# A decoder block: input projection as 22 Strassen pairs, then attention beside twelve gate blocks

## The chip, the core and the metric

The kernel runs on one core of a Trainium2 chip. Its engines work side by side and wait for each other by semaphores: TensorE (PE) multiplies matrices into PSUM, VectorE (DVE), ScalarE (ACT) and GpSimd (POOL) do the elementwise work, and SyncE (SP) issues DMAs. Each engine, and SP's queue, takes its instructions in a fixed row. The metric is the device time of one execution in microseconds; lower is better.

## The reference

One layer over 1040 positions (16 meta tokens and 1024 real ones), model width 1024, all in float32:

```python
h = xn @ w_in                                   # 1024 -> 8 * 1024
b_c, c_c, h_c, q, k, v, g_conv, g_attn = split(h)
y_conv = b_c * causal_dwconv(c_c * h_c, conv_w_mix)
z = q @ k.T / 8                                 # 16 heads of 64
log_beta = log_sigmoid(z)
log_fail = where(s < t, log_beta - z, 0)
survive = reverse_cumsum(log_fail) - log_fail
a = where(s < t, exp(log_beta + survive), 0)    # stick-breaking weights
o = a @ v
merged = sigmoid(g_conv + b0) * (y_conv @ w_proj_conv) \
       + sigmoid(g_attn + b1) * (o @ w_proj_attn)
x = x + rms_norm(merged @ w_out)
u, g = split(rms_norm(x) @ w_up_gate)
x = x + rms_norm((gelu(causal_dwconv(u)) * g) @ w_down)
```

A weight a[t,s] is beta(s) times the product of fail = 1 - beta over the positions between s and t. With P(s) the product of fail from s up, a[t,s] = P(s+1) - P(s), so o is also the sum over s of P(s) (v(s-1) - v(s)) plus the last v.

## The kernel before

Every float32 operand of a matmul is split into a high part (cast to float32r, by ACT) and a low part (the difference, by DVE or POOL), and a product is three matmuls: high x high, high x low, low x high. Weights come in blocks of 128 output features. A dense block (an *item* of `Dense`) loads its weights (`raw`), makes `whi` (ACT, L110) and `wlo` (POOL, four pieces, L113), and runs three chunks of about 342 tokens: 3 x 8 x 3 = 72 matmuls (L129 to L131) into a PSUM tile `mm`.

The input projection has 64 such items: 8 each of q, k, v, 24 of the convolution (c, h, b) and 16 gates. They are written between the steps of attention. `stage1` makes for each head and each block of 114 queries the scores (`z`, L330 and L331), two sigmoids (`fl` = fail, L332; `be` = beta, L333), the running product of `fail` (a scan on DVE, L340), beta times the product (POOL, L346) and the mask (POOL, L348). `stage2` transposes the weights (`tp`, L377), splits them (`ah` on ACT, `al` on DVE) and multiplies by v (`av`, L367 and L368). q, k and v of a head pair stay in SBUF. Two cost tables (`COST1`, `COST2`) and `marks` set how many dense steps stand between two steps of attention; what gates are left follow behind it. Then come the two branch projections (their inputs `yT` and `oT` are loaded from DRAM through a ring of two `ld` tiles and split), the output projection, the up/gate projection and the down projection.

The up/gate projection already works in Strassen form. Two weight blocks and both halves of the input dimension make a 2x2 block matrix, the even and odd tokens the other; with the operands A11, S1 to S4, A12, A22 of weights and B11, T1 to T4, B21, B22 of tokens there are seven products in place of eight. Its matmuls (L863, L865, L867) go into `st` tiles.

Of the kernel before, what the change touches and what calls it, by code (L numbers as in the profile page):

```python
# [1 line left out]

# [29 lines left out]

@with_exitstack
def block_kernel(ctx, tc, x, meta_tokens, g_pre_mix, w_in, channels, w_proj_conv,
# [23 lines left out]
    m_d = tc.dram_tile([D, NQ], F32, name="m_d")  # L58
    mm_d = tc.dram_tile([7, P, KB * QB], F32, name="mm_d")
# [4 lines left out]
    def split(hi, lo, src, lo_engine=None):  # L64
        nc.scalar.copy(hi, src)  # L65
        (lo_engine or nc.vector).tensor_tensor(lo, src, hi.bitcast(F32), op=ALU.subtract)  # L66

# [13 lines left out]
    class Dense:  # L81


        def __init__(self, pspool, items):
            self.ps = pspool
            self.items = items
            self.raw, self.hl = {}, {}
            self.i, self.gen, self.total, self.later = 0, None, 0, []

        def defer(self, n, fn):  # L90
            self.later.append((self.total + n, fn))

# [48 lines left out]
        def step(self):  # L141
            while self.i < len(self.items):
# [17 lines left out]
    def col_block(w, c):  # L160
# [51 lines left out]
    CH_C = [(T0 - 2, CH + 2), (T0 + CH, CH), (T0 + 2 * CH, CH)]  # L212
    CH_K = [(0, T0 + CH), (T0 + CH, CH), (T0 + 2 * CH, CH)]

    QH, QL, KK, V = {}, {}, {}, {}

    def item_q(p):
        def evac(ci, a, n, ps):
            if ci == 0:
                QH[p] = [heads.tile([P, NQ], F32R, name="qh", tag="qh") for _ in range(2)]  # L220
                QL[p] = [heads.tile([P, NQ], F32R, name="ql", tag="ql") for _ in range(2)]
                for h in range(2):
                    z0 = 64 * (1 - h)
                    nc.gpsimd.memset(QL[p][h][z0:z0 + 64, :].bitcast(F32), 0.0)
            c = slice(a - T0, a - T0 + n)
            for h in range(2):
                own, other = slice(64 * h, 64 * h + 64), slice(64 - 64 * h, 128 - 64 * h)
                hi, lo = QH[p][h], QL[p][h]
                nc.scalar.copy(hi[own, c], ps[own])
                nc.vector.tensor_copy(hi[other, c], ps[own])  # L230
                nc.vector.tensor_tensor(lo[own, c], ps[own], hi[own, c].bitcast(F32), op=ALU.subtract)
        return (col_block(w_in, 24 + p), src_x, CH_Q, evac)

    def item_k(p):
        def evac(ci, a, n, ps):
            if ci == 0:
                KK[p] = [heads.tile([P, NT], F32R, name="kk", tag="kk") for _ in range(2)]
            c = slice(a, a + n)
            for h in range(2):
                own, other = slice(64 * h, 64 * h + 64), slice(64 - 64 * h, 128 - 64 * h)  # L240
                k = KK[p][h]
                nc.scalar.copy(k[own, c], ps[own])
                nc.vector.tensor_tensor(k[other, c], ps[own], k[own, c].bitcast(F32), op=ALU.subtract)
        return (col_block(w_in, 32 + p), src_x, CH_K, evac)

    def item_v(p):
        st = {}

        def evac(ci, a, n, ps):
            if ci == 0:  # L250
                st["vt"] = work.tile([P, NT], F32, name="vt", tag="wk", bufs=4)
            vt = st["vt"]
            nc.scalar.copy(vt[:, a:a + n], ps)
            if ci < 2:
                return
            vv = heads.tile([P, 9, 2, P], F32R, name="vv", tag="vv", bufs=2)
            V[p] = vv

            def tokens(k0, kn, m):
                tp = ps_tp.tile([P, 512], F32, name="tp", tag="tp")  # L260
                for k in range(kn):
                    s0 = KEYS[k0 + k][0]
                    nc.tensor.transpose(tp[:m, k * P:(k + 1) * P], vt[:, s0:s0 + m], ident)
                tv = tp[:m, :kn * P].rearrange("p (k h d) -> p k h d", k=kn, h=2)
                split(vv[:m, k0:k0 + kn, :, 0:64], vv[:m, k0:k0 + kn, :, 64:128], tv)

            dense.defer(1, lambda: tokens(0, 4, P))
            dense.defer(2, lambda: tokens(4, 4, P))
            dense.defer(3, lambda: tokens(8, 1, QB))
        return (col_block(w_in, 40 + p), src_x, CH_K, evac)  # L270

    def items_conv(cb):
        st = {}

        def evac_c(ci, a, n, ps):
            if ci == 0:
                st["c"] = work.tile([P, NT], F32, name="cc", tag="wk", bufs=4)
            nc.scalar.copy(st["c"][:, a - 12:a - 12 + n], ps)

        def evac_h(ci, a, n, ps):  # L280
            c = st["c"][:, a - 12:a - 12 + n]
            nc.vector.tensor_tensor(c, c, ps, op=ALU.mult)
            if ci == 2:
                st["y"] = work.tile([P, NT], F32, name="yy", tag="wk", bufs=4)
                conv3(st["y"][:, :NQ], st["c"], NQ, lambda k: w_mix(k, cb))

        def evac_b(ci, a, n, ps):
            y = st["y"][:, a - T0:a - T0 + n]
            nc.vector.tensor_tensor(y, y, ps, op=ALU.mult)
            if ci == 2:  # L290
                nc.sync.dma_start(y_d[cb * P:(cb + 1) * P, :], st["y"][:, :NQ])

        return [(col_block(w_in, 8 + cb), src_x, CH_C, evac_c),
                (col_block(w_in, 16 + cb), src_x, CH_C, evac_h),
                (col_block(w_in, cb), src_x, CH_Q, evac_b)]
# [13 lines left out]
    gp = {"p": work, "n": 4}  # L309

    def gate_pool():
        return gp["p"]

    COST1, COST2 = (726.0, 1752.0, 2778.0), (1000.0, 1900.0, 2800.0)

    def stage1(p, h, g):
        res = []
        qh, ql, kk = QH[p][h], QL[p][h], KK[p][h]
        for b in range(3 * g, 3 * g + 3):
            nk = P + QB * b  # L320
            q0 = QB * b
            fl = work.tile([P, NT], F32, name="fl", tag="fl")[:QB]
            be = work.tile([P, NT], F32, name="be", tag="be", bufs=6)[:QB]
            nch = -(-nk // 512)
            wch = 2 * (-(-nk // (2 * nch)))
            c0 = 0
            while c0 < nk:
                n = min(wch, nk - c0)
                z = ps_z.tile([P, 512], F32, name="z", tag="z")[:QB, :n]
                nc.tensor.matmul(z, qh[:, q0:q0 + QB], kk[:, c0:c0 + n], start=True, stop=False)  # L330
                nc.tensor.matmul(z, ql[:, q0:q0 + QB], kk[:, c0:c0 + n], start=False, stop=True)  # L331
                nc.scalar.activation(fl[:, c0:c0 + n], z, AF.Sigmoid, scale=-0.125)  # L332
                nc.scalar.activation(be[:, c0:c0 + n], z, AF.Sigmoid, scale=0.125)  # L333
# [901 lines left out]
```

## Time and profile before

| | us |
|---|---|
| median of 3 runs | 2027.31 (2026.77 to 2027.63) |
| profiled execution | 2019.99 |
| its span | 2018.2 |
| PE busy | 1968.4 |
| DVE, ACT, POOL busy | 1006.3, 853.3, 1022.7 |
| first matmul of the first branch projection starts at | 1014.2 |

The span is that of one profiled execution. A busy time is the time in which an engine has an instruction under way; matmuls overlap, so a busy PE may still be waiting inside. A group's row reads: line, engine, operation, output <- inputs, shapes, count, then busy time and mean duration of one in ns, then the idle time of the engine before them and who ended it.

### The profile page before, as it was taken

The numbers are of one execution on the slowest core, as the hardware profiler recorded it, in microseconds if no ns is written. First come the engines' busy times: TensorE is split into PE (matmuls) and PEld (weight loads), VectorE is DVE, ScalarE is ACT, GpSimd is POOL, SyncE is SP. The second block draws the span as 40 slices with busy tenths as digits, with TensorE's granted clock in tenths as the row PEclk, the third lists the DMA queues.
The fourth block names the chain that finished last, engine by engine and source line by source line (L and its number), as shares of the span: only waits on it lengthen the run. The fifth ranks groups of instructions, "written<-read, shape, count | busy, mean of one in ns | idle before, by whom it ended". The sixth has DMA issues, their size and how long they took to land.

```text
span 2018.2 us, 30990 instructions
## 1 busy us (share of the span) xinstructions
PE 1968.4 (98%) x12228; PEld 1857.0 (92%) x12228; DVE 1006.3 (50%) x1545; ACT 853.3 (42%) x1771; POOL 1022.7 (51%) x1062
## 2 busy tenths in 40 slices
PE   6999999999999999999999999979999999999997
PEld 6999999999999999999999999969988998888886
DVE  6445555555555555553341126874354445345546
ACT  5544555555454545555421123453443344321122
POOL 2643666565555646565223550345556565654353
PEclk9999999999999999999999999989999999999998
DMA  3111101111111111012664673303121212253223
GB/s 137 43 63 43 53 32 64 43 53 43 42 53 43 58 39 62 32 64 73 189 221 156 188 214 114 97 31 126 63 84 67 102 66 82 92 174 111 84 84 136
DMA packets 56174, 177.58 MB, mean 88 GB/s; under 512 B 12872, under 2 KB 12872, under 8 KB 56028
## 3 DMA queue, kind: packets, MB, share of 16 engines
q1 hardware_dynamic: 52704, 165.09, 24.5%
q10 hardware_dynamic: 3324, 10.50, 1.7%
q8 instruction: 96, 1.57, 0.3%
q14 instruction: 50, 0.41, 0.1%
HBM read 131.36 MB, written 44.21 MB: 87 GB/s over the span
## 4 chain that ended last, share of the span: by engine, by line
PE 87%; DVE 7%; ACT 2%; DMA 2%; POOL 1%; issue 1%; ACTq 0%; DVEq 0%; SPq 0%; POOLq 0%
PE mm L129 14%; PE mm L130 14%; PE mm L131 14%; PE st L863 7%; PE st L867 7%; PE st L865 7%; PE tp L377 3%; PE st L1157 3%; PE st L1155 3%; PE st L1156 3%; PE av L368 2%; PE av L367 2%; PE z L331 2%; PE z L330 2%; PE po L706 1%; PE po L708 1%
## 5 line engine op out<-in xcount | busy, mean ns | idle before, releaser
L129 PE MATMUL mm<-xnT,whi 128*128 128x342 f32 (+2 forms) x1536 | 505.5, 329 | 0.3 <-ACT xnT L65 0.2
L130 PE MATMUL mm<-xnT,whi 128*128 128x342 f32 (+2 forms) x1536 | 494.0, 322 | 0.5 <-DVE xnT L66 0.5
L131 PE MATMUL mm<-xnT,wlo 128*128 128x342 f32 (+2 forms) x1536 | 492.3, 320 | 0.0
L346 POOL TENSOR_TENSOR be<-be,fl 114x271 f32<-114x271 f32 (+14 forms) x288 | 206.0, 736 | 310.3 <-DVE fl L340 301.6
L113 POOL TENSOR_TENSOR wlo<-raw,whi 128x256 fp32r<-128x256 f32 x320 | 254.8, 828 | 208.2 <-ACT whi L110 207.3
L130 PEld LDWEIGHTS mm<-xnT,whi 128*128 128x128 f32 x1536 | 291.0, 189 | 2.1 <-DVE xnT L66 1.0
L129 PEld LDWEIGHTS mm<-xnT,whi 128*128 128x128 f32 x1536 | 290.2, 189 | 2.9 <-ACT xnT L65 0.8
L131 PEld LDWEIGHTS mm<-xnT,wlo 128*128 128x128 f32 x1536 | 290.0, 189 | 0.0
L340 DVE TENSOR_TENSOR_SCAN fl<-fl,upper 114x128 f32<-114x128 f32 (+2 forms) x144 | 214.4, 1490 | 112.2 <-ACT fl L332 64.0
L66 POOL TENSOR_TENSOR a_op<-raw,a_op 128x512 fp32r<-128x512 f32 (+1 forms) x136 | 193.7, 1437 | 87.9 <-ACT a_op L65 85.6
L66 DVE TENSOR_TENSOR al<-tp,ah 114x342 fp32r<-114x342 f32 (+3 forms) x288 | 128.3, 452 | 148.8 <-ACT ah L65 147.5
L65 ACT CAST ah<-tp 114x342 fp32r<-114x342 f32 (+3 forms) x288 | 113.0, 398 | 165.3 <-PE tp L377 157.0
L863 PE MATMUL st<-opT,a_op 128*128 128x258 f32 (+2 forms) x528 | 172.3, 326 | 3.2 <-ACT snap L878 1.8
L865 PE MATMUL st<-opT,a_op 128*128 128x258 f32 (+2 forms) x528 | 170.1, 322 | 2.6 <-DVE opT L66 1.7
L867 PE MATMUL st<-opT,a_op 128*128 128x258 f32 (+2 forms) x528 | 170.0, 322 | 0.0
L332 ACT ACTIVATE fl<-z 114x348 f32<-114x348 f32 (+10 forms) x240 | 111.4, 464 | 123.6 <-PE z L331 93.5
L65 ACT CAST a_op<-raw 128x512 fp32r<-128x512 f32 (+1 forms) x136 | 85.1, 634 | 156.0 <-DMA raw<-in_w_up_gate_dram 51.8
L1162 DVE TENSOR_TENSOR acc<-acc,st 128x512 f32<-128x512 f32 x144 | 98.5, 687 | 91.1 <-PE st L1157 91.1
L865 PE MATMUL st<-opB,a_op 128*128 128x512 f32 (+2 forms) x396 | 127.6, 322 | 0.0
L863 PE MATMUL st<-opB,a_op 128*128 128x512 f32 (+2 forms) x396 | 127.6, 322 | 0.0
L867 PE MATMUL st<-opB,a_op 128*128 128x512 f32 (+2 forms) x396 | 127.2, 321 | 0.0
L377 PE MATMUL tp<-ident,be 114*114 114x114 f32 (+1 forms) x720 | 118.5, 262 | 4.1 <-DVE al L66 3.4
(168 smaller groups left out, 4320.5 us busy)
## 6 DMA issues: line engine op xcount, KB each, us to landing
raw<-in_w_in_dram SPq DMA_DIRECT2D x64, 512.0 KB, 3.3
raw<-in_w_up_gate_dram SPq DMA_DIRECT2D x44, 512.0 KB, 3.3
act_d<-owork SPq DMA_DIRECT2D x22, 512.0 KB, 4.3
araw<-act_d SPq DMA_DIRECT2D x22, 512.0 KB
raw<-in_w_down_dram SPq DMA_DIRECT2D x22, 512.0 KB, 3.3
y_d<-yy SPq DMA_DIRECT2D x8, 513.0 KB
ga_d<-gt SPq DMA_DIRECT2D x8, 513.0 KB
o_d<-ot SPq DMA_DIRECT2D x8, 513.0 KB
```

Of the source, the lines that this page charges most:

```text
L65: nc.scalar.copy(hi, src)
L66: (lo_engine or nc.vector).tensor_tensor(lo, src, hi.bitcast(F32), op=ALU.subtract)
L113: nc.gpsimd.tensor_tensor(lo[:, c], raw[:, c], hi[:, c].bitcast(F32), op=ALU.subtract)
L129: nc.tensor.matmul(ps, wh, xh, start=(kb == 0), stop=False)
L130: nc.tensor.matmul(ps, wh, xl, start=False, stop=False)
L131: nc.tensor.matmul(ps, wl, xh, start=False, stop=(kb == KB - 1))
L340: nc.vector.tensor_tensor_scan(fl[:, :nk][:, ::-1], fl[:, :nk][:, ::-1], upper[:, NT - nk:][:, ::-1], 1.0, op0=ALU.mult, op1=ALU.max)
L346: nc.gpsimd.tensor_tensor(be[:, a:e], be[:, a:e], fl[:, a + 1:e + 1], op=ALU.mult)
L377: nc.tensor.transpose(tp[:n, QB * j:QB * (j + 1)], blocks[j][0][:, k0:k0 + n], ident[:QB, :QB])
L863: nc.tensor.matmul(ps, wt[:, 0, k], xh, start=start and kb == 0, stop=False, skip_group_check=True)
L865: nc.tensor.matmul(ps, wt[:, 0, k], xl, start=False, stop=False, skip_group_check=True)
L867: nc.tensor.matmul(ps, wt[:, 1, k], xh, start=False, stop=stop and kb == 3, skip_group_check=True)
```

## The change

Three parts, all ahead of the branch projections.

1. *A Strassen stage.* After the norm and five plain blocks, 44 of the 64 blocks run as 22 pairs, in two halves of 260 tokens. The token operands T1 to T4 are made once (`tops`); B11, B21, B22 are parts of `xnT`. q, k and v are stored to DRAM as high and low parts. v is turned into differences v(s-1) - v(s) (`dv`) and transposed; the last v of each query block is kept in `ends`.
2. *Attention beside 12 gate blocks.* Heads load q, k (64 partitions at a time) and v from DRAM, three heads ahead at most. Scores, one sigmoid, the scan, transposes of the scan itself, split, products with the differences, and at the end an addition of `ends`. Beta, its product and the mask are gone. Two gates (`late_gates`) follow as `Dense` items while the eight `y` blocks are loaded.
3. *A list scheduler.* Each step is a task of `Plan` with an engine, a cost, a key and the slots that it takes and frees; `run` writes them out in the order in which they would start. `in_program_order` keeps that order on every engine.

```diff
+class Plan:
+    LAG = {"PE": 0.22, "ACT": 0.1, "DVE": 0.1, "POOL": 0.1, "SP": 3.5, None: 0.0}
...
+    plan = Plan({"raw": 2, "whi": 0, "wlo": 0, "ap": 4, "wk": 5, "st": 8, "xw": 2})
...
+            h = plan.add("ACT", act_cost(n), high, tuple(after), key + 3, ("wk",))
+            t = plan.add("DVE", dve_cost(n), lower, (h,), key + 4)
+            s1 = plan.add("SP", 0.4, lambda: nc.sync.dma_start(hi_d[rows, :], st["hi"].bitcast(F32)), (h,), key + 4)
...
+            nc.vector.tensor_tensor(st["dv"][:, 1:], u()[:, :NT - 1], u()[:, 1:], op=ALU.subtract)
...
+                for kb in range(4):
+                    c = slice(kb * P, (kb + 1) * P)
+                    xh, xl = token_op(tok, kb, s * HS, HS)
+                    nc.tensor.matmul(ps, wt[:, 0, c], xh, start=start and kb == 0, stop=False,
+                                     skip_group_check=True)
+                    nc.tensor.matmul(ps, wt[:, 0, c], xl, start=False, stop=False, skip_group_check=True)
+                    nc.tensor.matmul(ps, wt[:, 1, c], xh, start=False, stop=kb == 3, skip_group_check=True)
...
+    FL = [2] * 6 + [1] * 3
+    plan = Plan({"raw": 2, "whi": 1, "wlo": 1, "mm": 2, "z": 2, "tp": 3, "av": 1, "qk": 3, "vv": 2,
+                 "ot": 2, "wk": 2, "ah": 4, "al": 4, "half": 1, **{f"fl{b}": n for b, n in enumerate(FL)}})
...
+    share = {0: 0.18, 1: 0.33, 2: 0.49}
...
+    DELAY = 0.6 * half_pair
...
+                            nc.scalar.activation(bst["fl"][:, c0:c0 + n], bst["z", c0], AF.Sigmoid,
+                                                 scale=-0.125)
...
+                        nc.vector.tensor_tensor_scan(fl[:, ::-1], fl[:, ::-1], upper[:, NT - nk:][:, ::-1],
+                                                     1.0, op0=ALU.mult, op1=ALU.max)
...
+                            nc.tensor.transpose(tp[:n, QB * j:QB * (j + 1)], fls[b]["fl"][:, k0:k0 + n],
+                                                ident[:QB, :QB])
...
+            nc.gpsimd.tensor_tensor(ov, ov, ends[:, p].unsqueeze(2).to_broadcast([P, 9, QB]), op=ALU.add)
...
+    items = [item_gate(0, ob) for ob in late_gates]
-                    nc.gpsimd.tensor_tensor(be[:, a:e], be[:, a:e], fl[:, a + 1:e + 1],
-                                            op=ALU.mult)
```

How the rows of instructions move, at three places. First PE, in the middle of the input projection. Before, dense matmuls of 342 columns stand with a pair of scores (`z`) between them:

```order
L330 MATMUL z<-kk,qh 114x470
L331 MATMUL z<-kk,ql 114x470
L129 MATMUL mm<-xnT,whi 128x342
L130 MATMUL mm<-xnT,whi 128x342
L131 MATMUL mm<-xnT,wlo 128x342
```

In the change, PE's row there holds only Strassen products of 260 columns; the place is the step from B22 (a part of `xnT`) to T4 (`tT_504`) as the token operand:

```order
L776 MATMUL st<-xnT,s_op 128x260
L778 MATMUL st<-xnT,s_op 128x260
L779 MATMUL st<-xnT,s_op 128x260
L776 MATMUL st<-tT_504,s_op 128x260
L778 MATMUL st<-tT_504,s_op 128x260
L779 MATMUL st<-tT_504,s_op 128x260
```

No score, transpose of weights or weighted sum is left in that part of the row. Second, DVE inside attention. Before, the scans (`fl`) and the low parts (`al`) stand among the splits of q that the projection needs:

```order
L340 SCALAR_TENSOR_TENSOR fl<-fl,upper 114x698
L66 TENSOR_TENSOR al<-tp,ah 128x342
L66 TENSOR_TENSOR al<-tp,ah 114x228
L230 CAST qh<-mm 64x342
L231 TENSOR_TENSOR ql<-mm,qh 64x342
L66 TENSOR_TENSOR al<-tp,ah 114x114
```

In the change, near the end of attention, DVE's row has nothing but these two kinds:

```order
L975 SCALAR_TENSOR_TENSOR fl<-fl,upper 114x698
L429 TENSOR_TENSOR al<-tp,ah 114x342 x2
L429 TENSOR_TENSOR al<-tp,ah 114x228
L975 SCALAR_TENSOR_TENSOR fl<-fl,upper 114x812
L429 TENSOR_TENSOR al<-tp,ah 114x114
L429 TENSOR_TENSOR al<-tp,ah 128x342
L975 SCALAR_TENSOR_TENSOR fl<-fl,upper 114x926
```

The splits of q and k have moved into the stage before. Third, PE at the end of attention. Before, three dense matmuls stand behind each transpose and its pair of weighted sums:

```order
L377 MATMUL tp<-ident,be 114x114 x3
L367 MATMUL av<-ah,vv 128x342
L368 MATMUL av<-al,vv 128x342
L129 MATMUL mm<-xnT,whi 128x342
L130 MATMUL mm<-xnT,whi 128x342
L131 MATMUL mm<-xnT,wlo 128x342
```

In the change the last of the twelve gates has ended some hundred rows earlier, and single matmuls of the next gate stand between:

```order
L994 MATMUL tp<-ident,fl 114x114 x6
L1009 MATMUL av<-ah,vv 128x342
L1010 MATMUL av<-al,vv 128x342
L994 MATMUL tp<-ident,fl 114x114 x2
L1009 MATMUL av<-ah,vv 128x342
L233 MATMUL mm<-xnT,wlo 128x342
L1010 MATMUL av<-al,vv 128x342
L994 MATMUL tp<-ident,fl 114x114
```

The dense matmuls that stood beside the last units of attention now stand ahead of them, or behind.

More of the change, by code (lines that the diff above doesn't have):

```diff
@@ L246, in item_v @@
[L246 to L295, printed above, removed]
+    HT = NT // 2
@@ L414, in block_kernel, with plain_step @@
[L414 to L431 removed]
+    def plain_step(ps, hi, lo, kb, a, n):
+        k = slice(kb * P, (kb + 1) * P)
+        xh, xl = src_x(kb, a, n)
+        nc.tensor.matmul(ps, hi[:, k], xh, start=(kb == 0), stop=False)
+        nc.tensor.matmul(ps, hi[:, k], xl, start=False, stop=False)
+        nc.tensor.matmul(ps, lo[:, k], xh, start=False, stop=(kb == KB - 1))
@@ new lines, in block_kernel, with load_raw, whole @@
+    ends = xnt_pool.tile([P, NPAIR, 9], F32, name="ends")
+    gates = [(1, ob) for ob in range(8)] + [(0, ob) for ob in range(8)]
+    N_FIRST, N_LATE = 1, 2
+    strassen_gate, bridge_gate = gates[0], gates[1]
+    mid_gates = gates[2:16 - N_LATE]
+    late_gates = [ob for _, ob in gates[16 - N_LATE:]]
+    def load_raw(o):
+        raw = wpool.tile([P, D], F32, name="raw", tag="raw")
+        nc.sync.dma_start(raw, w_in[o])
+        return raw
+    def whole(raw):
+        hi = wpool.tile([P, D], F32R, name="whi", tag="whi")
+        lo = wpool.tile([P, D], F32R, name="wlo", tag="wlo")
+        return hi, lo
@@ new lines, in late_tile, with plain_out, make, evac @@
+    def late_tile(u):
+        return lambda: u["t"]
+    def plain_out(done, k, t0):
+        u = {}
+        def make():
+            u["t"] = wk_tile("su")
+        def evac(a, n, ps):
+            nc.scalar.copy(u["t"][:, a:a + n], ps)
+        return make, evac, lambda after, key: done(k, late_tile(u), after, key)
+    done_q, done_k = done_qk(qh_d, ql_d, T0), done_qk(kh_d, kl_d, 0)
+    block = {}
+    for k in range(8):
+        block["v", k] = (40 + k, k, done_v)
+        block["q", k] = (24 + k, k, done_q)
+        block["k", k] = (32 + k, k, done_k)
+        block["c", k] = (8 + k, k, done_c)
+        block["h", k] = (16 + k, k, done_h)
+        block["b", k] = (k, k, done_b)
@@ new lines, in block_kernel @@
+    at = 0.0
+    item = 24 * 3 * pe_cost(CH)
+    for i, name in enumerate((("v", 0), ("q", 0))):
+        u = {"t": first_out[i]}
+        o, k, done = block[name]
+        plain(o, CH_K, at, None, lambda a, n, ps, u=u: nc.scalar.copy(u["t"][:, a:a + n], ps),
+              lambda after, key, done=done, k=k, u=u: done(k, late_tile(u), after, key), bank,
+              2, (*first_ops[i], None))
+        at += item / 3
+    for name in (("k", 0), ("v", 1), ("q", 1)):
+        o, k, done = block[name]
+        plain(o, CH_K, at, *plain_out(done, k, 0), bank)
+        at += item
@@ new lines, in block_kernel, with gate_out, make, evac @@
+    snap_free = {}
+    for i in range(len(pairs1)):
+        strassen_pair(i, at)
+        at += 14 * prod
+    def gate_out(which, ob, tile_of, space):
+        u = {}
+        def make():
+            u["t"] = tile_of()
+        def evac(a, n, ps):
+            nc.scalar.activation(u["t"][:, a - T0:a - T0 + n], ps, AF.Sigmoid, bias=bias_gate(which, ob))
+        def finish(after, key):
+            plan.add("SP", 0.4, lambda: nc.sync.dma_start(
+                (gc_d, ga_d)[which][ob * P:(ob + 1) * P, :], u["t"][:, :NQ]), tuple(after), key, (), space)
+        return make, evac, finish
@@ new lines, in block_kernel, with next_load, next_high @@
+    which, ob = bridge_gate
+    plain(48 + 8 * which + ob, CH_Q, at, *gate_out(which, ob, lambda: wk_tile("gt"), ("wk",)), bank)
+    at += item
+    nxt = {}
+    which, ob = mid_gates[0]
+    def next_load():
+        nxt["raw"] = load_raw(48 + 8 * which + ob)
+    def next_high():
+        nxt["hi"], nxt["lo"] = whole(nxt["raw"])
+        nc.scalar.copy(nxt["hi"], nxt["raw"])
+    ld = plan.add("SP", 0.4, next_load, (), at - 20, ("raw",))
+    h = plan.add("ACT", act_cost(D), next_high, (ld,), at - 10, ("whi", "wlo"))
@@ new lines, in block_kernel @@
+    plan.join([plan.add("POOL", pool_cost(256), lambda j=j: lo_piece(nxt["raw"], nxt["hi"], nxt["lo"], j),
+                        (h,), at - 9) for j in range(4)], ("raw",))
+    plan.run()
+    psS.close()
+    t_ctx.close()
+    early_ctx.close()
+    psA = ctx.enter_context(ExitStack())
+    ps_mm = psA.enter_context(pool("ps_mm", 2, space=PSUM))
+    ps_z = psA.enter_context(pool("ps_z", 2, space=PSUM))
+    ps_tp = psA.enter_context(pool("ps_tp", 3, space=PSUM))
+    ps_av = psA.enter_context(pool("ps_av", 1, space=PSUM))
@@ L540, in block_kernel @@
+    plan.run()
+    last = len(nc.cur_bb.bb.instructions)
+    psA.close()
+    work_ctx.close()
+    heads_ctx.close()
+    psB0 = ctx.enter_context(ExitStack())
+    items = [item_gate(0, ob) for ob in late_gates]
+    n_gates = len(items)
+    dense = Dense(psB0.enter_context(pool("ps_mmB", 3, space=PSUM)), items)
     slots_abc = ctx.enter_context(ExitStack())
```

814 lines of the change are left out of this document (590 added, 224 removed).

## The prediction, as it stood before the run

> **What bounds the kernel now.** I read the page's busy shares and its chain first, then the stages by windows, then the groups that the change touches.
>
> ```profile
> PE 1968.4 (98%) x12228; PEld 1857.0 (92%) x12228; DVE 1006.3 (50%) x1545; ACT 853.3 (42%) x1771; POOL 1022.7 (51%) x1062
> PE 87%; DVE 7%; ACT 2%; DMA 2%; POOL 1%; issue 1%; ACTq 0%; DVEq 0%; SPq 0%; POOLq 0%
> ```
>
> TensorE is busy 98% of the span and carries 87% of the chain that ended last. The windows (span from:to, length, then busy time and count of PE, PE's weight loads, DVE, ACT, POOL, then clock, DMA share, GB/s) say where:
>
> ```profile
> 0.00:45.00 45.00, 29.14 (x170) 26.61 (x170) 30.52 (x77) 25.57 (x54) 11.18 (x19) 1.00 0.43 154
> 45.00:925.00 880.00, 874.52 (x5782) 855.48 (x5781) 471.35 (x685) 454.75 (x1037) 499.81 (x654) 1.00 0.14 49
> 925.00:970.00 45.00, 44.54 (x299) 43.62 (x298) 17.64 (x25) 21.41 (x46) 22.21 (x28) 1.00 0.19 68
> 970.00:1014.00 44.00, 44.00 (x282) 44.00 (x281) 11.93 (x24) 18.56 (x40) 11.54 (x16) 1.00 0.75 226
> 1340.00:1770.00 430.00, 426.89 (x2645) 381.66 (x2645) 194.68 (x233) 179.29 (x305) 248.28 (x180) 1.00 0.24 85
> ```
>
> From 45 to 1014 us, all of the input projection and the attention, PE idles 6 us (5.5 + 0.5). So only fewer PE cycles can make this part shorter; work taken off DVE, ACT or POOL there is worth nothing by itself. The last row is the up/gate projection, already in Strassen form: 22 pairs, and PE idles 3.1 us in 430. It is the model for the new stage.
>
> **Removed and added PE work.** A matmul's listed duration overlaps the next one's, so I price by the distance of starts:
>
> ```profile
> 1000.04 0.32 PE L129 MATMUL mm<-xnT,whi 128*128 128x342 f32 x1
> 1007.89 0.32 PE L131 MATMUL mm<-xnT,wlo 128*128 128x342 f32 x1
> 1499.76 0.28 PE L863 MATMUL st<-opB,a_op 128*128 128x256 f32 x1
> 1504.34 0.28 PE L867 MATMUL st<-opT,a_op 128*128 128x256 f32 x1
> L129 PE MATMUL mm<-xnT,whi 128*128 128x342 f32 (+2 forms) x1536 | 505.5, 329 | 0.3 <-ACT xnT L65 0.2
> ```
>
> Between the first two rows lie 50 steps: 7.85/50 = 0.157 us for 342 columns. Between the next two lie 38: 4.58/38 = 0.1205 us for 256. The slope, 0.0365/86 = 0.0004 us a column, gives 0.122 us for 260. Three lines of 1536 matmuls are 64 blocks of 72. Of these, 44 go: 3168 x 0.157 = 497.4 us, and 2 us more, since key and value blocks have 14 extra columns in their first chunk. In come 22 pairs x 7 products x 2 halves x 12 = 3696 matmuls of 260 columns: 3696 x 0.122 = 451 us (bounds 445 at the 256-column price, 455 with 1 ns more each). PE saving: **48 us** (44 to 54).
>
> The Trainium skill ("TensorE: Matmul & The Clock Gate", Back-to-back issue gap) gives N/2.4 + 2.5 ns for an isolated warm stream, 145 and 111 ns here; by it the saving would be 459 - 410 = 49 us. The trace's pitches are 8 to 10% longer, and they are used.
>
> Transposes, scores and weighted sums keep their counts (720, 480, 576), so they cancel. Their size is still needed. Busy time to 1014 is 29.1 + 874.5 + 44.5 + 44.0 = 992; less the blocks (4608 x 0.157 + 2 = 725) that is 267. About 15 us of it are the 144 other transposes at the 0.105 us found below, so attention's PE work is some 250 us, and the new attention stage with its 12 gate blocks (12 x 72 x 0.157 = 136) has **386 us** for PE.
>
> **Work on other engines.**
>
> ```profile
> L346 POOL TENSOR_TENSOR be<-be,fl 114x271 f32<-114x271 f32 (+14 forms) x288 | 206.0, 736 | 310.3 <-DVE fl L340 301.6
> L333 ACT ACTIVATE be<-z 114x348 f32<-114x348 f32 (+10 forms) x240 | 110.6, 461 | 0.0
> L348 POOL TENSOR_SCALAR_AFFINE_SELECT be<-be 114x114 f32<-114x114 f32 x144 | 113.6, 789 | 10.1
> L340 DVE TENSOR_TENSOR_SCAN fl<-fl,upper 114x128 f32<-114x128 f32 (+2 forms) x144 | 214.4, 1490 | 112.2 <-ACT fl L332 64.0
> L66 DVE TENSOR_TENSOR al<-tp,ah 114x342 fp32r<-114x342 f32 (+3 forms) x288 | 128.3, 452 | 148.8 <-ACT ah L65 147.5
> L113 POOL TENSOR_TENSOR wlo<-raw,whi 128x256 fp32r<-128x256 f32 x320 | 254.8, 828 | 208.2 <-ACT whi L110 207.3
> ```
>
> The second sigmoid (110.6 us on ACT), the multiplication and the mask (206.0 + 113.6 us on POOL) go, replaced by differences of v and a sum of ends. Directly that is worth 0: PE hid them. Indirectly it is what lets attention fit beside 386 us of PE. There DVE keeps scans and low parts, 214.4 + 128.3 = 343 us: 89% of the stage, where its share was 54% (471 of 880).
>
> *Strassen stage.* Each pair asks of POOL seven low parts and of DVE four combinations and six evacuations, as in the model stage, plus the q/k/v splits and the convolution. The model's PE waits were 3.1 us; I take 4 (3 to 12: the convolution and splits share the ring of output tiles, and a late store would hold an evacuation). The token operands T1 to T4 are made under 264 plain matmuls, 264 x 0.157 = 41 us; nearly free.
>
> *Attention stage.* The old one idled 5.5 us in 880, with DVE at 54%. At the same rate 386 us would lose 2.4 us; at 89% there is little slack when a scan is late, and the queue behind it is the low part that releases a transpose bank, for which PE waits. I take 8 (2 to 30).
>
> *q/k/v through DRAM.* Head 0's six loads wait for the last T4 product. Until the first score PE has 72 + 39 = 111 gate matmuls, 17.4 us.
>
> ```profile
> L553 SPq DMA_DIRECT2D ld<-y_d x8: 319/320/424, 973.4 to 997.4; - x8
> DMA to landing us min/median/max: 4.6/5.6/6.7
> L65 ACT CAST yT<-ld x24: 473/477/480, 978.7 to 1003.1; 128x342 fp32r<-128x342 f32 x24
> L129 PE MATMUL mm<-yT,whi x192: 315/318/327, 1014.2 to 1103.9; 128*128 128x342 f32 x192
> ```
>
> Six issues of 0.32 and a landing of 5.6 are 7.5 us; on SP they stand behind the last store of the Strassen gate, a few us more. Hidden, unless the gate block ahead of them runs short; I take 2 for all the joints (0 to 10). Later heads have three buffers.
>
> *The end of attention.* Before, gate matmuls stand between all of its last products. Now, after the last mid gate, PE's row has 11 score pairs, 66 transposes, 27 weighted pairs and seven strays of the next gate. DVE has seven scans and 26 low parts.
>
> ```profile
> 890.65 0.32 PE L131 MATMUL mm<-xnT,wlo 128*128 128x342 f32 x1
> 890.81 0.46 PE L377 MATMUL tp<-ident,be 114*128 114x114 f32 x3
> 891.04 0.40 PE L129 MATMUL mm<-xnT,whi 128*128 128x342 f32 x1
> 891.28 0.32 PE L130 MATMUL mm<-xnT,whi 128*128 128x342 f32 x1
> L340 DVE TENSOR_TENSOR_SCAN fl<-fl,upper 114x1040 f32<-114x1040 f32 x16 | 40.1, 2508 | 16.3 <-POOL be L346 9.7 <-ACT fl L332 6.5
> L340 DVE TENSOR_TENSOR_SCAN fl<-fl,upper 114x356 f32<-114x356 f32 x16 | 17.5, 1092 | 8.9 <-ACT fl L332 8.9
> ```
>
> Two dense matmuls and three transposes take 0.63 us, so a transpose is (0.63 - 0.314)/3 = 0.105. PE: 66 x 0.105 = 6.9, scores of 9772 columns 4.5, weighted sums 7.3, strays 1.1: 19.8 us. DVE: scans between 1.09 and 2.51, about 1.8 x 7 = 12.6, and 26 x 0.452 = 11.8: 24.4 us, and some 2 us from the last low part to the last sum. PE idles 24.4 + 2 - 19.8 = **7 us** (3 to 17; the upper end is half a microsecond of waiting for ACT before each of 20 low parts).
>
> *The projection behind it.* The eight y blocks took from 973.4 to about 1004.4, 31 us, under five gate blocks. Now only two gates (21.5 us after the strays) stand behind attention. Two loads are issued early (one landing saved, 6); the others stand on SP behind the last store of o, which waits for POOL's last addition (4 more). Ready at 31 - 6 + 4 = 29; PE needs the last block at 21.5 + 7 x 3 x 0.157 = 24.8. Wait: **5 us** (0 to 12).
>
> **Sum.** -48 (PE work) - 6 (old idle) + 4 + 8 + 2 + 7 + 5 = **-28 us**. The profiled execution took 2019.99 (span 2018.2), 7.3 below the median of 2027.31; the same difference goes to the median: **2000 us**.
>
> **Rivals.**
> - *The waits hide.* Strassen 3, attention 2, tail 3, the rest 0: -54 + 8 = -46, 1981 us. For it: PE's 0.6% idle in the old mix. Against it: the old mix kept dense matmuls to the end.
> - *The joints are dearer.* Tail 12, y 10, joints 8 in place of 14: -12, 2015 us. For it: where PE last ran beside a DVE chain, its clock fell too:
>
> ```profile
> 1310.00:1330.00 20.00, 11.43 (x66) 10.67 (x67) 16.98 (x28) 8.71 (x14) 3.29 (x2) 0.74 0.08 24
> ```
>
>   PE busy 57% had a granted clock of 0.74. The Trainium skill ("TensorE: Matmul & The Clock Gate", Part 1: The HAM clock gate) says that an idle window of about 3.4 us halves the clock; 925 to 970 shows none, the next tail may.
> - *Slower: DVE becomes the bound by waiting in its row.* In the old kernel it waited 147.5 us for ACT's high parts. If its fixed row in the new stage keeps these waits, the stage takes 343 + 147.5 = 490 us against 386 + 8: +96 - 28 = +68, 2095 us. It decides from 343 + waits > 394 + 28, that is 79 us of waits. Against it: there DVE had nothing else to do, and scans now stand between.
> - *Slower: POOL locks DVE out.* POOL has 44 weight pieces x 0.83, 48 half additions and 8 last ones, some 105 us by the same rate per column. Taken one after the other with DVE: 343 + 105 = 448, +54 - 28 = +26, 2053 us. Such delays are in the rows already, with POOL at 57% (500 of 880), where it now has 27%. The Trainium skill ("SBUF — State Buffer", Who interferes with whom) has a lock between a DVE operation with two SBUF inputs, as the scan is, and a GpSimd operation that reads SBUF; the low parts, one input from PSUM, are outside it.
>
> **Chances.** Forecast (1988 to 2008) 0.45, waits hide 0.22, dearer joints 0.21, DVE bound 0.07, lock 0.05. What counts as no change is within 0.2%, 4 us. Faster: 0.45 + 0.22 + 0.18 of the joints = 0.85; same 0.04; slower 0.11. The range reaches from below the hidden case to beyond the joints, 1976 to 2024, and leaves out the two slower rivals and a little at each end.
>
> **What would show it.** A 22-pair stretch of some 455 us with PE idle under 12; an attention stretch of 390 to 405 us with DVE near 85% busy; 5 to 10 us of PE gaps at its end; PE waiting for yT at the first projection block; this block starting near 986 instead of 1014. PE waits on al or fl spread over the whole attention stretch, or scans much above 1.5 us on average, would make the prediction wrong.

## The result, and the profile after

The changed kernel takes 2015.35 us (median of 4 runs, 2014.96 to 2017.75), the kernel before 2027.04 (4 runs, 2025.46 to 2027.63): a ratio of 0.9946, 95% interval 0.9929 to 0.9963. It is faster by 11.7 us where 28 were forecast; 2015 was the time of the rival with dearer joints. The profiled execution took 2014.96 (span 2012.9).

The page's busy shares and its chain, after:

```profile
PE 1921.6 (95%) x12756; PEld 1806.6 (90%) x12756; DVE 1089.6 (54%) x1585; ACT 842.1 (42%) x1774; POOL 907.7 (45%) x676
PE 73%; DVE 12%; ACT 3%; POOL 3%; DMA 2%; issue 2%; ACTq 0%; DVEq 0%; SPq 0%; POOLq 0%
```

TensorE's share fell from 98% to 95%: there is less work for it, and it waits more. DVE has gone from 7% to 12% of the chain. The stages by windows (span, length, then busy time and count of PE, weight loads, DVE, ACT, POOL, clock, DMA share, GB/s); 585.6 is the first score, 981.3 the last weighted sum, 1003.0 the first projection matmul:

```profile
0.00:45.00 45.00, 28.98 (x171) 27.01 (x172) 28.75 (x74) 25.00 (x54) 7.38 (x15) 1.00 0.42 154
45.00:585.60 540.60, 517.48 (x4142) 514.77 (x4141) 268.23 (x320) 208.26 (x424) 292.16 (x208) 0.98 0.36 111
585.60:981.30 395.70, 375.94 (x2610) 357.12 (x2608) 310.83 (x432) 261.82 (x669) 124.92 (x102) 1.00 0.49 128
981.30:1003.00 21.70, 21.70 (x140) 21.70 (x140) 5.65 (x12) 9.10 (x20) 5.66 (x6) 1.00 0.62 174
```

PE idles 540.6 - 517.5 = 23.1 us up to attention and 395.7 - 375.9 = 19.8 in it. Who ended those waits, up to the first score (engine, line, waited for: total, times, longest):

```profile
PE st L776 <- ACT tT L638: 8.1, 1, 8.1
PE st L569 <- DVE dv L553: 4.7, 1, 4.7
PE st L776 <- ACT snap_e L786: 4.5, 6, 0.9
PE st L331 <- ACT whi L439: 2.5, 1, 2.5
PE st L333 <- POOL wlo L354: 2.5, 1, 2.5
PE st L778 <- POOL tT L429: 0.8, 1, 0.8
```

and from there to the projection:

```profile
PE av L1010 <- DVE al L429: 11.4, 20, 1.8
PE tp L994 <- DVE al L429: 6.0, 6, 1.3
PE mm L231 <- ACT yT L158: 2.6, 1, 2.6
```

The first table is the surprise: 4.5 us in it are the running Strassen stage, waiting for snapshots. The other 18.6 are one place, between 52 and 103 us, where the token operands T1 to T4 are made. Two of these waits (`whi`, `wlo`, 5.0) are still in the plain blocks; ACT and POOL have casts and low parts of token operands ahead of them in their rows. Then PE, three quarters through its first product with T1, waits 8.1 + 0.8 for T1's last quarter, and 4.7 for `dv`.

The cause stands in DVE's row:

```profile
44.72 4.62 DVE L612 TENSOR_TENSOR xa<-xnT 128x1040 f32<-128x1040 f32 x2
49.27 3.53 DVE L162 TENSOR_TENSOR xa<-xa 128x520 f32<-128x520 f32 x2
```

and in POOL's, at the same time:

```profile
44.88 6.75 POOL L617 TENSOR_TENSOR xb<-xnT 128x1040 f32<-128x1040 f32 x2 [24.68 <-DVE xnT L159]
```

Two additions of 1040 columns take DVE 4.62 us and POOL 6.75 beside each other. Later in the same row a single one takes DVE 1.23 (at 92.64, with POOL idle). A subtraction of 520 columns takes 0.69 where POOL is idle as it starts and 1.2 to 2.8 where it is not. In all, DVE's 28 operations on token operands take 38 us, where 4 x 1.23 + 24 x 0.69 make 21.5. And DVE stands still for POOL, 6.0 us in three waits for low parts, of which POOL makes one in 1.3 us where it is alone:

```profile
DVE xa L162 <- POOL tT L429: 6.0, 3, 2.5
```

The cover is shorter than planned, too. Line L331 has one of every three plain matmuls here:

```profile
44.00:83.50 39.50, 21.36 (x64) 12.45 (x64) 0.91 0.24 83
121.34 0.33 PE L331 MATMUL st<-xnT,whi 128*128 128x356 f32 x1
```

Only 3 x 64 = 192 of the 264 plain matmuls run before the first Strassen product at 83.5; the last plain block starts at 121.3, when the operands are done. The cover was 30 us and not 41. The long wait has a price of its own, in the column for the clock (third from the end) of windows of 4 us:

```profile
96.00:100.00 4.00, 1.18 (x3) 0.58 (x3) 2.74 (x5) 2.11 (x5) 1.80 (x2) 0.50 0.00 0
...
104.00:108.00 4.00, 4.00 (x26) 4.00 (x25) 0.00 (x0) 0.75 (x2) 0.05 (x1) 0.69 0.41 131
```

After 8 us without work the granted clock is 0.50, and it is back at 1.00 only from 108 on; in the last row 26 matmuls ran where 4 us at full pitch hold 33, about 0.8 us lost. The Trainium skill ("TensorE: Matmul & The Clock Gate", Part 1: The HAM clock gate) gives the halved clock after an idle window of about 3.4 us; the 0.50 agrees.

### The profile page after: what moved, and what is told of

It reads as the page before. It is cut to its first block, busy times and chain, and to the rows that moved or that the text cites. A ratio compares the mean times of both kernels' runs of the same rounds, so it can differ in the third digit from the quotient of the medians.

```text
span 2012.9 us, 32307 instructions
## 1 busy us (share of the span) xinstructions
PE 1921.6 (95%) x12756; PEld 1806.6 (90%) x12756; DVE 1089.6 (54%) x1585; ACT 842.1 (42%) x1774; POOL 907.7 (45%) x676
## 4 chain that ended last, share of the span: by engine, by line
PE 73%; DVE 12%; ACT 3%; POOL 3%; DMA 2%; issue 2%; ACTq 0%; DVEq 0%; SPq 0%; POOLq 0%
PE st L1396 7%; PE st L1398 7%; PE st L1400 7%; PE st L776 7%; PE st L779 7%; PE st L778 7%; DVE fl L975 4%; PE st L1690 3%; PE st L1688 3%; PE st L1689 3%; PE mm L231 2%; PE tp L994 2%; PE mm L233 2%; PE mm L232 2%; PE mm L331 2%
## 5 line engine op out<-in xcount | busy, mean ns | idle before, releaser
L429 POOL TENSOR_TENSOR s_op<-raw,s_op 128x512 fp32r<-128x512 f32 x132 | 184.3, 1399 | 153.3 <-ACT s_op L731 150.6
L975 DVE TENSOR_TENSOR_SCAN fl<-fl,upper 114x128 f32<-114x128 f32 (+3 forms) x144 | 207.4, 1451 | 48.4 <-ACT fl L964 47.9
L776 PE MATMUL st<-tT,s_op 128*128 128x260 f32 x704 | 201.5, 286 | 12.7 <-ACT tT L638 8.1
L778 PE MATMUL st<-tT,s_op 128*128 128x260 f32 x704 | 199.9, 284 | 0.8 <-POOL tT L429 0.8
L779 PE MATMUL st<-tT,s_op 128*128 128x260 f32 x704 | 199.6, 284 | 0.0
L162 DVE TENSOR_TENSOR raw<-raw 128x512 f32<-128x512 f32 x88 | 95.6, 1086 | 141.8 <-POOL a_op L159 106.8
L1039 POOL TENSOR_TENSOR ot<-ot,half 64x342 f32<-64x342 f32 x48 | 63.3, 1318 | 211.1 <-ACT ot L1035 199.8
L731 ACT CAST s_op<-raw 128x512 fp32r<-128x512 f32 x132 | 82.1, 623 | 161.9 <-PE st L779 100.8
L776 PE MATMUL st<-xnT,s_op 128*128 128x260 f32 x528 | 149.2, 283 | 0.0
L779 PE MATMUL st<-xnT,s_op 128*128 128x260 f32 x528 | 149.0, 282 | 0.0
L778 PE MATMUL st<-xnT,s_op 128*128 128x260 f32 x528 | 148.6, 281 | 0.0
L429 DVE TENSOR_TENSOR al<-tp,ah 114x342 fp32r<-114x342 f32 (+3 forms) x288 | 117.8, 440 | 53.5 <-ACT ah L999 52.4
L776 PEld LDWEIGHTS st<-tT,s_op 128*128 128x128 f32 x704 | 133.0, 189 | 14.1 <-ACT tT L638 8.3
L999 ACT CAST ah<-tp 114x342 fp32r<-114x342 f32 (+3 forms) x288 | 108.0, 401 | 73.7 <-PE tp L994 69.0
L778 PEld LDWEIGHTS st<-tT,s_op 128*128 128x128 f32 x704 | 133.1, 189 | 1.1 <-POOL tT L429 1.1
L779 PEld LDWEIGHTS st<-tT,s_op 128*128 128x128 f32 x704 | 133.5, 190 | 0.0
```

Source lines behind the costliest of these rows:

```text
L162: engine.tensor_tensor(out, a, b, op=ALU.subtract)
L429: eng.tensor_tensor(out, src, hi.bitcast(F32), op=ALU.subtract)
L776: nc.tensor.matmul(ps, wt[:, 0, c], xh, start=start and kb == 0, stop=False, skip_group_check=True)
L778: nc.tensor.matmul(ps, wt[:, 0, c], xl, start=False, stop=False, skip_group_check=True)
L779: nc.tensor.matmul(ps, wt[:, 1, c], xh, start=False, stop=kb == 3, skip_group_check=True)
L975: nc.vector.tensor_tensor_scan(fl[:, ::-1], fl[:, ::-1], upper[:, NT - nk:][:, ::-1], 1.0, op0=ALU.mult, op1=ALU.max)
```

## Experiments: the token operands

Ratios are against the kernel before, run again beside each group of experiments: medians of 2025.25, 2026.81 and 2026.1. Differences of 2 us between groups therefore mean little.

**1. More cover.** Two of the Strassen blocks run as plain blocks in front:

```diff
+    plain(48 + 8 * which + ob, CH_Q, at, *gate_out(which, ob, lambda: wk_tile("gt"), ("wk",)), bank)
...
+    plain(o, CH_K, at, *plain_out(done, k, 0), bank)     # block ("k", 7)
...
-              ("v", 7), ("q", 7), ("k", 7)]              # and the gate, the last pair
+              ("v", 7), ("q", 7)]
```

> 21 Strassen pairs, and the last pair's two blocks (a gate and the last k) run as plain blocks in front: seven plain blocks cover the token operands in place of five. PE work grows by 22.6 - 20.5 = 2.1 us. Theory (the token operands are late, 18.6 us of PE waits between 60 and 104 us): 22.6 us more cover takes away 13 to 18 of these waits, time 1999 to 2004 against 2015.35. Rival (the operands take longer as more low parts of weights run beside them on POOL): only half of it goes, about 2008. Rival (these waits only move to another place): 2017.

Measured: 2017.35 (12 runs, ratio to before 0.9964, 0.9949 to 0.9979). No gain. PE's waits up to the first scores:

```profile
PE st L569 <- DVE dv L553: 9.1, 1, 9.1
PE st L794 <- ACT snap_e L804: 4.5, 6, 0.9
PE z L963 <- DMA ql<-ql_d: 3.1, 1, 3.1
```

The wait for T1 (8.9) is gone, as expected. That for `dv`, which stands ahead of 108 of the 144 added matmuls in PE's row, grew from 4.7 to 9.1, the 5.0 in front (`whi`, `wlo`) stayed, and at the first scores PE waits 3.1 for head 0's loads; another pair is now last, and in experiment 3, with the conv pairs last, this wait is gone. With 2.1 more PE work that is no gain: the third reading, the waits moved. Cover helps only the waits that stand behind it in the row.

**2. The operands on one engine.** All work on them that POOL had goes to DVE:

```diff
-            nc.gpsimd.tensor_tensor(st["b"], xnT[:, 0, kb + 4].bitcast(F32), ...
+            nc.vector.tensor_tensor(st["b"], xnT[:, 0, kb + 4].bitcast(F32), ...
...
-        ("T1", "o1", "o1", "e1", "POOL"), ... ("T3", "e1", "o1", "e1", "POOL")
+        ("T1", "o1", "o1", "e1", "DVE"), ... ("T3", "e1", "o1", "e1", "DVE")
```

> POOL's share of the token operands (four additions of 1040, eight low parts of 520) goes to DVE. Theory (DVE and POOL, both reading two SBUF operands, stretch each other): DVE has some 10 us more at undisturbed rates (4 x 1.23 + 8 x 0.61), but its 520-column operations fall from 1.2 to 2.8 us back to 0.69 where POOL is quiet; the first product with T4 comes at 85 to 92 us, waits in front of 110 us fall from 18.6 to under 8, time 2003 to 2008. Rival (there is simply too much work in DVE's row): the operands come 10 us later, waits 28, time 2025.

Measured: 2008.36 (6 runs, ratio 0.9917, 0.9900 to 0.9934), 7.0 less than the changed kernel and just above the theory's 2008. DVE's row at the same place:

```profile
44.63 1.23 DVE L612 TENSOR_TENSOR xa<-xnT 128x1040 f32<-128x1040 f32 x1
45.78 1.23 DVE L617 TENSOR_TENSOR xb<-xnT 128x1040 f32<-128x1040 f32 x1
...
53.94 1.22 DVE L162 TENSOR_TENSOR xa<-xa 128x520 f32<-128x520 f32 x1
```

DVE does four additions and eight low parts more and is done sooner, at 94.3 us in place of 101.5. Its first addition takes 1.23 us, where two took 4.62; all 40 operations take 39 us, where 28 took 38; and it no longer waits for POOL. From 49 us on, POOL makes low parts of weights, and 520 columns are at 1.2 again. The mean of eight `xa` subtractions fell from 1.42 to 0.89 us. PE's waits up to 140 us went from 18.6 to 9.8, not quite to the 8 expected:

```profile
PE st L569 <- DVE dv L553: 6.8, 1, 6.8
PE st L776 <- DVE vt L429: 3.0, 1, 3.0
```

So the operands were late because two engines made them, side by side and in turn, and not because DVE had too much to do. The run takes the stretching and the waits for POOL's own, slower work away together; how much of the 7.0 us each is worth stays open. For the stretching, the Trainium skill ("SBUF — State Buffer", Who interferes with whom) has this rule, a DVE operation with two SBUF inputs against a GpSimd operation that reads SBUF; the prediction weighed it for attention only, and the runs show it here first.

**3. One engine and more cover.** Experiments 1 and 2 together, with the last conv pairs moved to the stage's end.

> Token operands wholly on DVE, and seven plain blocks in front (the gate and the last k, 21 pairs; the last conv pairs now stand last of the stage). Theory (once DVE and POOL no longer stretch each other, 22.6 us more cover is enough): the 9.8 us of waits left at the operands (6.8 for dv, 3.0 behind it) go to 0 to 2, PE work +2.1, time 2008.4 - 9 + 2 = 2000 to 2003. Rival (DVE's row is simply long, waits for dv move with the cover as in the run with seven plain blocks alone): waits of 8 to 10 stay, 2009 to 2012.

Measured: 2006.77 (6 runs, ratio 0.9907, 0.9890 to 0.9924). The time lies between theory and rival, and the waits are the rival's: the 3.0 fell to 0.2, but that for `dv` stayed at 7.8. ACT's row in experiment 2 shows why:

```profile
82.71 0.62 ACT L638 CAST tT<-xa 128x520 fp32r<-128x520 f32 x1 [2.98 <-DVE xa L162]
83.25 0.44 ACT L663 COPY su<-st 128x342 f32<-128x342 f32 x1
85.09 0.62 ACT L638 CAST tT<-xa 128x520 fp32r<-128x520 f32 x1 [1.41 <-DVE xa L162]
...
86.84 0.44 ACT L663 COPY su<-st 128x342 f32<-128x342 f32 x1
```

The copy of the second v block's last chunk (`su`, 86.84) stands behind casts of token operands, and those wait for DVE (2.98 and 1.41). DVE makes `dv` from that copy, and PE's row has the transposes of `dv` ahead of the added blocks and of the products.

**4. No Strassen.** The 44 blocks as plain blocks, no token operands:

```diff
-    for i in range(len(pairs1)):
-        strassen_pair(i, at)
...
+    for name in order:
+        o, k, done = block[name]
+        plain(o, CH_K, at, *plain_out(done, k, 0), bank)
```

> The 44 Strassen blocks run as plain blocks in the same stage, the token operands are not made; q, k, v through DRAM and attention as in the changed kernel. PE work +48. Theory (the Strassen stage pays 48 us and gives back 18.6 at the token operands and 4.5 at snapshots): 2015.35 + 48 - 23 = 2040. Rival (the lost time lies in the attention stage and stays, Strassen pays its 48 in full): 2063. Both read the rest of the change (q/k/v through DRAM, the new attention stage) as this time less 2027: +13 or +36.

Measured: 2048.93 (4 runs, ratio 1.0123, 1.0101 to 1.0146), 33.6 more than with Strassen. The window up to the first score:

```profile
45.00:618.00 573.00, 571.53 (x3611) 571.11 (x3610) 81.34 (x72) 151.85 (x253) 195.20 (x218) 1.00 0.39 114
```

PE is busy 571.5 us in place of 517.5. That is 54 more: the 48 forecast, and some 4 because all but one of the blocks run over 1040 tokens here (43 x 24 matmuls x 14 columns x 0.0004 = 6, of which the forecast had 2); 2 stay open. It idles 1.5 in place of 23.1, so the first score comes 32.4 later, and the time is 33.6 longer. The time lies 9 above the theory's and 14 under the rival's, but the trace is clear: Strassen spares PE 54 us here (50 without the added columns) and gives 21.6 of them back in its own stage. Read as the expectation has it, the rest of the change (q, k and v through DRAM, the new attention stage) is a loss: 2048.93 is 23.7 us above the 2025.25 of the kernel before, and some 4 of these are the added columns.

## Experiments: attention

**5. No additions on POOL.** They are left out.

```diff
-plan.add("POOL", pool_cost(CH), out3, (o1, o2), ...
+plan.add("POOL", pool_cost(CH), None, (o1, o2), ...
...
-fin = plan.add("POOL", pool_cost(NQ), last_add, ...
+fin = plan.add("POOL", pool_cost(NQ), None, ...
```

> Attention without POOL's additions (48 of the two halves, 8 of the ends): they are left out, so o lacks one half and the ends; all other work stays, PE's row is the same. Theory (a POOL addition beside a scan stretches it, and the low parts behind it come late): all sixteen 1040-column scans take 2.3 to 2.5 us (now five take 3.3 to 4.0), PE's waits in the attention stage fall from 19.8 to about 13, time 2008 to 2011. Rival (the waits come from the order in which the planner wrote DVE's row): scans shorter, waits still 18 to 20, time 2014 to 2016.

Measured: 2007.94 (4 runs, ratio 0.9916, 0.9894 to 0.9937). The longest scans in the changed kernel, and then without the additions:

```profile
L975 DVE TENSOR_TENSOR_SCAN fl<-fl,upper 114x1040 f32<-114x1040 f32 x16 | 42.8, 2677 | 1.2 <-ACT fl L964 1.2
```

```profile
L975 DVE TENSOR_TENSOR_SCAN fl<-fl,upper 114x1040 f32<-114x1040 f32 x16 | 37.1, 2316 | 1.2 <-ACT fl L964 1.2
```

(Four of the sixteen were stretched, to 3.5 to 4.0 us; the expectation's fifth is a row of two scans.) What such a meeting does, in the changed kernel:

```profile
649.38 1.91 POOL L1052 TENSOR_TENSOR ot<-ot,ends 128x1026 f32<-128x1026 f32 x1
...
649.47 3.99 DVE L975 TENSOR_TENSOR_SCAN fl<-fl,upper 114x1040 f32<-114x1040 f32 x1 [0.20 <-ACT fl L964]
...
651.24 2.92 POOL L1039 TENSOR_TENSOR ot<-ot,half 64x342 f32<-64x342 f32 x1
...
653.92 0.42 PE L1010 MATMUL av<-al,vv 114*128 114x342 f32 x1 [1.75 <-DVE al L429]
```

POOL's two additions lie beside the scan, it takes 3.99 us in place of 2.32, the low parts behind it are late, and PE waits 1.75. The stage from first score to last sum, without the additions:

```profile
585.00:972.40 387.40, 372.50 (x2609) 355.76 (x2608) 302.78 (x432) 261.56 (x669) 49.32 (x48) 1.00 0.50 130
```

387.4 in place of 395.7, with 14.9 us idle in place of 19.8. The time came out as expected, though the idle time fell less: the other 3.4 us lie inside PE's busy time, where short waits don't show. The waits that remain are not those of POOL's additions; POOL still makes low parts of weights there, 49.3 us.

**6. The additions on other engines**, nothing left out:

```diff
+nc.vector.tensor_tensor(o, ust["av"][a0:a0 + 64], ust["half"][a0:a0 + 64], op=ALU.add)   # 48, from PSUM
...
+nc.scalar.activation(o, o, AF.Identity, bias=ends[:, p, b:b + 1])                        # 72
...
-nc.gpsimd.tensor_tensor(o, o, ust["half"][a0:a0 + 64], op=ALU.add)
```

> Nothing is left out of attention: the two halves are added by DVE straight from PSUM (48 of about 0.45 us, in place of ACT's copy and POOL's addition), the ends by ACT as a bias (72 of 114 columns). Theory (POOL's additions beside the scans cost 8 us): scans of 1040 columns all at 2.3 us, 21.6 us more in DVE's row cost 0 to 4 us of new waits, attention stage 388 to 392 us in place of 395.7, time 2008 to 2012. Rival (DVE is the bound by its row): its 340 us in 388 bring back what the scans gave, PE's waits 20 or more, time 2014 to 2020.

Measured: 2017.68 (8 runs, ratio 0.9961, 0.9947 to 0.9974): the rival. The stage's window, first score to last sum:

```profile
585.60:984.50 398.90, 377.45 (x2611) 357.77 (x2610) 324.67 (x479) 264.27 (x691) 42.88 (x48) 1.00 0.49 126
```

DVE and ACT have 14 and 2 us more, and PE idles 21.5. The longest scans are back at 2.3 us and PE's waits for `al` fall from 17.4 to 11.2, but new ones stand beside them: 6.5 for ACT's `fl` (none before) and 2.5 for DVE's `ot`. What the scans gave, the longer rows took back. Put into the kernel of experiment 3:

> The two together. Theory (two separate places, so the gains add): waits at the operands 0 to 2, attention stage 388 to 392, time 1993 to 1999. Rival (what is gained ahead is lost again at the first projection or behind it, where y and o are awaited): 2002 to 2008.

Measured: 2007.64 (6 runs), against 2006.77 without it. That is in the rival's range, but not for its reason: PE waits 3.5 for `yT` there, and 4.2 without this part; this part simply gains nothing there either.

**7. A looser order.** The scheduler of attention is told that results are seen later:

```diff
+    Plan.LAG = {"PE": 0.4, "ACT": 0.25, "DVE": 0.25, "POOL": 0.1, "SP": 3.5, None: 0.0}   # was 0.22, 0.1, 0.1
```

> In attention the scheduler assumes that a result is seen later by others (PE 0.4, ACT and DVE 0.25 us in place of 0.22 and 0.1); nothing else changes. Theory (of the 19.8 us of waits in the attention stage the part that is not POOL's comes from an order written for results that are there sooner than the chip has them): waits for al fall from 17.4 to under 10, time 2006 to 2010. Rival (these waits come from stretched scans and locks alone): 17 us stay, 2014 to 2016. A longer stage (over 2017) would say that the order was already right.

Measured: 2001.17 (4 runs, ratio 0.9881, 0.9864 to 0.9899): 14.2 less than the changed kernel by the order of instructions alone, and 5 below the theory's range. The stage's window, and then PE's waits from 600 us to the projection:

```profile
585.90:964.60 378.70, 369.76 (x2609) 356.16 (x2607) 311.72 (x432) 260.12 (x669) 119.36 (x102) 1.00 0.53 133
```

```profile
PE av L1011 <- DVE al L429: 7.0, 10, 2.0
PE mm L231 <- ACT yT L158: 4.0, 3, 2.5
PE tp L995 <- DVE al L429: 1.2, 1, 1.2
```

The stage takes 378.7, 17 less. The waits for `al` fell from 17.4 to 8.2. PE's busy time fell too, from 375.9 to 369.8 with the same matmuls (2610 and 2609 in the records): as in experiment 5, it seems that waits too short to be listed stood inside it. DVE is busy 311 and 312 us, and the long scans still take 2.6 on average.

**8. Both.** The looser order, with POOL's additions left out:

> Attention without POOL's additions (left out as before: o lacks one half and the ends) and with the larger lags, no other change. If stretched scans and an order written too tightly are two separate losses, they add: 2001.2 - 7.4 = 1994. If the slack of the new order already takes up the stretched scans, 1999 to 2002.

Measured: 1994.52 (4 runs, 1992.7 to 1998.51): by the medians the two add. The trace says otherwise. The stage's window:

```profile
585.90:961.70 375.80, 368.55 (x2608) 357.35 (x2607) 304.41 (x432) 260.45 (x669) 44.73 (x48) 1.00 0.53 134
```

The stage gains 2.9 us, not 8.3, so there the looser order seems to take up most of what stretched scans cost. PE's waits for `yT`, whose loads stand behind the last store of o, fall from 4.0 to 2.3. The profiled execution is the slowest of the four and 3.8 under that of experiment 7, where the medians are 6.7 apart; which of the two readings holds stays open.

## Experiments: the better kernel

**9.** Experiment 2 with the looser order:

> Token operands wholly on DVE, and the larger lags in attention's scheduler. Theory (two separate losses): 2008.4 - 14.2 = 1994 (1991 to 1997). Rival (what attention gains is lost where y is awaited): wait for yT over 8 us in place of 4, time about 2000.

Measured: 1988.88 (4 runs, ratio 0.9815, 0.9801 to 0.9830), on the theory's side and 2 us below its range. PE waits 4.4 for `yT`, not the rival's 8. Why the two together give 5 us more than their sum was not looked into.

**10.** Experiment 3 with the looser order, and the transposes of the second v block moved behind the plain blocks:

```diff
-t = plan.add("PE", 0.11 * kn, turn, (f,), key + 6, ("st",))
+t = plan.add("PE", 0.11 * kn, turn, (f,), key + (60 if p == 1 else 6), ("st",))
```

> The kernel with seven plain blocks and the operands on DVE, with the transposes of the second v block keyed 54 us later, so that they stand behind the plain blocks in PE's row, and the larger lags in attention. Theory (the 7.8 us wait was for those transposes alone: the copy of v's last chunk stood in ACT's row behind casts of token operands that wait for DVE): the wait is gone and nothing takes its place, 2006.8 - 7.8 - 14.2 = 1985 (1983 to 1989). Rival (PE then waits at the first T product for the last operands): 5 to 8 us stay, 1990 to 1993.

Measured: 1984.86 (5 runs, ratio 0.9795, 0.9782 to 0.9809). PE's waits up to 570 us:

```profile
PE st L331 <- ACT whi L439: 4.7, 1, 4.7
PE st L795 <- ACT snap_e L805: 3.7, 5, 1.0
PE st L333 <- POOL wlo L354: 0.3, 1, 0.3
```

The wait for `dv` is gone, and so are those for T1. The 5.0 for weights are others than in the changed kernel: 4.7 of them come at 107.5 us, in a plain block written behind the first Strassen products, for a high part that ACT makes late because it waits 1.84 us for the raw weights to land.

**11.** The looser order in the Strassen stage too:

> As the run with late transposes, and the scheduler of the Strassen stage has the larger lags too. Theory (an order for later results also spares the waits for snapshots): 3.7 to 4.5 us of snapshot waits go to under 1, 1981 to 1985. Rival (those waits are set by the ring of operands, not by the order): no change against the run with late transposes, within 2 us.

Measured: 1983.76 (4 runs, 1979.25 to 1987.63), within the spread of experiment 10. The snapshot waits stayed at 3.7, so the order's lags don't set them, as the rival has it; whether the ring of operands does was not tried.

The kernel of experiment 10 beats the one before by 41 us and the changed one by 30, with the same work in attention and 21 Strassen pairs in place of 22.

## Why the prediction was off, step by step

The steps against the traces, up to the end of the wait for `yT` (1003.0 + 3.1 against 1014.2, which is the same -8.1):

| term | forecast | measured |
|---|---|---|
| PE work | -48 | 944.1 - 992.2 = -48.1 |
| old idle time | -6 | -6 |
| joints: token operands, loads | +2 | +18.6, +0 |
| Strassen stage | +4 | +4.5 |
| attention, spread and end | +8, +7 | +19.8 in all, some 3.5 of it at the end |
| wait for yT | +5 | +3.1 |
| sum | -28 | -8.1 |

- *The step that failed* is "The token operands T1 to T4 are made under 264 plain matmuls, 264 x 0.157 = 41 us; nearly free". It named a cover and not the work under it, and it did not count the cover in PE's row. Listed out, DVE has 28 operations there and POOL 12; stretched by each other and waiting for each other, with other blocks' operations between them, they fill 44 to 102 us. Of the cover, 192 matmuls (30 us) stand ahead of the first product. The waits there are 18.6 us, and they were put at nothing. Even with the whole 2 for the joints set against them, that is 17 of the 20 us by which the sum was off, and outside the joints' bound of 10. The mechanism stood in the prediction as a rival ("POOL locks DVE out"), at another place.
- *Attention*: 15 forecast, 19.8 measured, inside the bounds. The reason given, a DVE 89% busy whose late scans hold up low parts, is half right: DVE is busy 310.8 of 395.7 us, 79%, and an order of instructions for slightly later results makes the stage 17 us shorter with the same DVE. The forecast took the order as given and did not ask which latencies it was written for. One of its own signs of being wrong, waits on `al` spread over the whole stage, is there: 5.1, 3.6, 3.8 and 4.9 us in four stretches of 100 us from 585 on.
- *The end of attention*: DVE's 24 us against PE's 20 gave 7; the listed waits after 961 us add to 3.5.
- *PE work, old idle time, the running Strassen stage, yT* came out within 2 us. That the PE work fell by 48.1 against a forecast of 48 is in part luck. The 260 columns, never timed before, start 0.120 us apart (100 steps from 299.81 to 311.83 us) and not 0.122, which makes the products 7 us cheaper; and in the order of experiment 7 the same work up to the projection is busy 938.2 us, 54.0 less than before. The difference is attention's busy time, 375.9 against 369.8, so the changed kernel's seems to hold waits that hide the cheaper products. The stretch from the first Strassen product to the last took 484.6 where 455 were forecast: 444 for the products, 18.1 of waits, v's transposes (63 x 0.105 = 6.6) and the 72 plain matmuls of the late block (11.3), both left out of the 455, make 480; 4 stay open.
- *Behind the first projection matmul* code and work are the same, yet it took 1009.9 us after and 1004.0 before; 3.1 is the wait for `yT`. The other kernels here took 1009 to 1016 there, and the profiled execution of before lay 7 under its median. So the profiled executions differ by 5.0 and the medians by 11.7. That it was a quick one of a kernel whose runs spread from 2019 to 2031 would fit; it is not shown.
- *The rivals.* The time is that of the dearer joints, 2015, but its terms were 12 for the tail, 10 for `yT` and 8 for the joints; measured are 3.5, 3.1 and 18.6. The joints were dearer, the other two were not; that the number is hit is luck. The lock's price has a slip: at 0.83 us for 256 columns, 44 weight pieces and 48 x 342 + 8 x 1026 columns of additions are 116 us and not 105, which makes that rival 2064 and not 2053. Attention took 395.7 us, not the 448 or 459 of that rival.

## What to carry to other kernels

Work "under" other work must be listed engine by engine with its durations, and the cover counted in the row as it is written. Two elementwise engines that both read two SBUF operands were worth little more than one here: two additions each took DVE 4.62 us in place of 2.46 and POOL 6.75 in place of some 4.9 (2.43 for one with DVE idle for most of it, in experiment 1). Cover helps only what stands behind it in the waiting engine's row; the row decides, not the amount. Where a scheduler fixes the order, a few tenths of a microsecond in its assumed latencies can be worth more than an engine's load: try them first, they cost one line.

## Hardware: what was not expected

A DVE operation beside POOL does not get longer evenly: 520 columns mostly took 0.69, 1.23 or 1.77 us, steps of 0.54 (up to 2.80 once), and 1040-column scans 2.3 to 2.5 or 3.5 to 4.0. POOL's operations lengthen too (an addition of 64 x 342 takes 0.93 us in the median and up to 2.94). DVE operations with one input in PSUM did not: the 288 low parts `al` took 0.24 to 0.52 us throughout, with POOL busy or not. And PE's busy time holds waits of its own: the same row of some 2610 matmuls was busy 375.9 us with POOL's additions and 372.5 without them, and in the looser order 369.8.
